# The states' output stage of a hybrid encoder layer: its u and Toeplitz loads by four groups into four buffers

## The chip, the core and the metric

The kernel runs on one core of a Trainium2 chip. A core has five engines that run side by side, each with its own stream of instructions: TensorE (PE, matrix products; PEld are its weight loads), VectorE (DVE), ScalarE (ACT), GpSimd (POOL) and SyncE (SP). Transfers between the chip's main memory and the on-chip memory go through 16 DMA engines that all of the core's queues share. POOL, SP and ACT issue them; each has a queue of its own. The metric is the device time of one execution in microseconds (us).

## The reference

One encoder layer over two sequences of 512 tokens with 1024 channels, all in float32. Two branches start from the same normalised rows: a windowed attention, and a state-space branch (S5) with 64 groups of 16 channels and 64 complex states per group and direction. A merge and an MLP follow.

```
h = rms_norm(x, ln1)
q, k, v, u, g_att, g_ssm = split(h @ w_in)
y_att = windowed_attention(rms_norm(q), rms_norm(k), v, sink, bias, mask)
# per direction d and group g, a linear recurrence over the tokens:
#   state[l] = a * state[l-1] + b_bar @ u[l];   y[l] = Re(c @ state[l])
y = y_forward + y_backward + d_skip * u
y = gelu(y);  y_ssm = y * sigmoid(y @ w_glu + b_glu)
mixed = sigmoid(g_att) * y_att + sigmoid(g_ssm) * y_ssm
x = x + mixed @ w_out
out = x + square(relu(rms_norm(x, ln2) @ w_up)) @ w_down
```

## The kernel before

The kernel is one long program for one core. Most of its time goes into matrix products, written as three products of split operands. The state-space branch works in blocks of 8 tokens. Within a block, the output follows from the inputs through a Toeplitz block per group (128 x 128); what comes from earlier blocks goes through the states at the block's edge. So the branch has three stages:

1. Coefficients. `tables` makes, by 8 groups, the tables `ct_scr` (from states to outputs) and the lags of the Toeplitz blocks, and stores them in main memory. Eight transfers (L595) build `toep_scr` from the lags.
2. The recurrence over the blocks, on DVE (L619 to L625). PE meanwhile works on the columns of the input projection; `pull` takes so many units of them at a time.
3. The states' output stage (L644 to L673), which the change is about. It has 32 steps `q` of `SH` = 2 groups. For each group, PE multiplies the Toeplitz block `toep` with the inputs `u_sb` (L655) and adds two products of the table `ctab` with the states `st` (L658). ACT applies the GELU (L665) and stores the outputs by four groups (L640). Behind each step, `pull` puts some matmuls of the projection (L185) or of the keys (L225) on PE.

Three kinds of tiles are loaded from main memory for the output stage, all issued by POOL. `u_sb` (L601) and `toep` (L603) are loaded for `SB` = 8 groups at a time, 512 KB each, into two buffers each. `ctab_in` (L609) is loaded for `SI` = 4 groups, 512 KB, into three buffers. Two of the first kind and three of the second are loaded ahead of the recurrence (L613 to L615). Behind them stands a copy of 4 MB in main memory, `line_scr` (L616), for the attention's biases. In the loop, a load is asked for when the last step that uses its buffer has been written (L670 to L673). I call the four groups of one `ctab` a set: it has two steps, and there are 16.

The orders of PE, ACT and DVE in this stage are those in which the code is written (`manual_schedule`, L618). POOL isn't among them there: a scheduler sets its order. A load waits until PE has read what stood in its buffer, and until an older transfer of POOL's queue that used the same semaphore (there are eight, in turn) has landed. Behind these loads on POOL stand the key norms, L238 and L239, on which DVE's L242 waits.

Of the kernel before, what the change touches and what calls it, by code (L numbers as in the profile page):

```python
# [12 lines left out]
F32 = mybir.dt.float32  # L13
# [6 lines left out]
P = 128  # L20
# [5 lines left out]
NSEQ = 2  # L26
# [12 lines left out]
GROUPS = 64  # L39
STATE = 64  # L40
CH = 16
T = 8
NCHUNK = SEQ // T
SB = 8
SI = 4
SG = 4
SH = 2
# [16 lines left out]
def hybrid_layer(ctx, tc, x, rel, onehot, w_qkv, w_ug, vectors, lam, coefs, w_glu, w_out, ln2,  # L64
                 w_up, w_down, out):
    nc = tc.nc
    V, S, PE, GP, SP = nc.vector, nc.scalar, nc.tensor, nc.gpsimd, nc.sync
# [18 lines left out]
    def sps():  # L86
        return ps_s.tile([P, 512], F32, tag="sps", name="sps")

    u_scr = dram.tile([GROUPS, CH, T, NSEQ * NCHUNK], F32, name="u_scr")
# [3 lines left out]
    toep_scr = dram.tile([CH, T, GROUPS, T * CH], F32, name="toep_scr")  # L93
# [173 lines left out]
    def pull(units):  # L267
        while units > 0:
            cost = next(filler, None)
            if cost is None:  # L270
                return
            units -= cost
            phase["units"] -= cost
# [175 lines left out]
    with tc.tile_pool(name="hst", bufs=1) as hp:  # L449
# [147 lines left out]
        with tc.tile_pool(name="ssmo", bufs=2) as sp:  # L597
            def load_batch(g0):

                u_sb = sp.tile([P, SB, NSEQ * NCHUNK], F32, tag="u_sb", name="u_sb")  # L600
                GP.dma_start(u_sb, u_scr[g0:g0 + SB].rearrange("g c t k -> (c t) g k"))  # L601
                toep = sp.tile([P, SB, T, CH], F32, tag="toep", name="toep")
                GP.dma_start(toep.rearrange("p g t c -> p g (t c)"),  # L603
                             toep_scr[:, :, g0:g0 + SB].rearrange("c t g n -> (c t) g n"))
                return u_sb, toep

            def load_table(g0):
                ctab = sp.tile([P, SI, 2, T * CH], F32, tag="ctab", name="ctab_in", bufs=3)
                GP.dma_start(ctab.rearrange("p g r n -> p (g r n)"),  # L609
                             ct_scr[:, g0:g0 + SI].rearrange("p g r n -> p (g r n)"))  # L610
                return ctab

            ahead = [load_batch(0)]  # L613
            ahead_c = [load_table(0), load_table(SI), load_table(2 * SI)]
            ahead.append(load_batch(SB))  # L615
            GP.dma_start(line_scr, line_one[:, None, :].to_broadcast([N_HEADS, P, LINE]))  # L616
            order.close()
            order.enter_context(tc.manual_schedule(engines={mybir.EngineType.PE, mybir.EngineType.Activation, mybir.EngineType.DVE}))  # L618
            for i in range(1, NCHUNK - 1):  # L619
                t1, t2 = [sp.tile([P, 2, GROUPS, NSEQ], F32, tag="st", name=n, bufs=3) for n in ("t1", "t2")]  # L620
                V.tensor_mul(t1, h[:, i], a8r)
                V.tensor_mul(t2, h[:, i, ::-1], a8i)
                V.tensor_add(t1, t1, h[:, i + 1])
                V.tensor_add(h[:, i + 1], t1, t2)
                pull(15)  # L625
            phase["gelu"] = True
            pull(64)
            def state_rows(q):
                st = sp.tile([P, 2, SH, NSEQ, NCHUNK], F32, tag="st", name="st", bufs=3)
                hv = h[:, :, :, q * SH:(q + 1) * SH, :].rearrange("p k r g s -> p r (g s) k")  # L630
                sv = st.rearrange("p r g s k -> p r (g s) k")
                V.tensor_copy(sv[64:128], hv[64:128, :, :, ::-1])
                if q % 2 == 0:
                    S.copy(sv[0:64], hv[0:64])
                else:
                    V.tensor_copy(sv[0:64], hv[0:64])
                return st

            def store_y(y, ga):
                S.dma_start(y_scr[:, :, ga:ga + SI].rearrange("t c g k -> (t c) (g k)"), y.rearrange("p g k -> p (g k)"))  # L640

            states = [state_rows(0), state_rows(1)]
            full = None
            for q in range(GROUPS // SH):  # L644
                g0 = q * SH
                if g0 % SB == 0:
                    u_sb, toep = ahead.pop(0)
                if g0 % SI == 0:
                    ctab = ahead_c.pop(0)
                    ys = sp.tile([P, SI, NSEQ * NCHUNK], F32, tag="ys", name="ys", bufs=3)  # L650
                st = states.pop(0)
                ps = sps()
                for g in range(SH):
                    o = ps[:, g * P:(g + 1) * P]
                    PE.matmul(o, toep[:, g0 % SB + g].rearrange("p t c -> p (t c)"), u_sb[:, g0 % SB + g, :],  # L655
                              start=True, stop=False)
                    for ri in range(2):
                        PE.matmul(o, ctab[:, g0 % SI + g, ri, 0:T * CH],  # L658
                                  st[:, ri, g].rearrange("p s k -> p (s k)"), start=False, stop=ri == 1)
                if q + 2 < GROUPS // SH:  # L660
                    states.append(state_rows(q + 2))
                if full:
                    store_y(*full)
                    full = None
                S.activation(ys[:, g0 % SI:g0 % SI + SH].rearrange("p g k -> p (g k)"), ps[:, 0:SH * P], AF.Gelu_apprx_tanh)  # L665
                if (g0 + SH) % SI == 0:
                    full = ys, g0 + SH - SI

                pull(-(-(phase["units"] - 84) // (GROUPS // SH - q)))
                if (g0 + SH) % SI == 0 and g0 + SH + 2 * SI < GROUPS:  # L670
                    ahead_c.append(load_table(g0 + SH + 2 * SI))
                if (g0 + SH) % SB == 0 and g0 + SH + SB < GROUPS:
                    ahead.append(load_batch(g0 + SH + SB))  # L673
            store_y(*full)
            pull(phase["units"])
            order.close()
# [67 lines left out]
    with tc.tile_pool(name="att", bufs=2, reuse_waits="tile") as ap, tc.tile_pool(name="attc", bufs=1, reuse_waits="tile") as ac:  # L744
# [293 lines left out]
        with tc.manual_schedule(engines={ET.PE, ET.Activation, ET.DVE, ET.Pool}):  # L1038
            for i, (j, sq) in enumerate(steps):
# [4 lines left out]
                for qb in range(NB):  # L1044
                    if 1 <= i < 3:
                        t = (i - 1) * NB + qb
# [599 lines left out]
```

## Time and profile before

| what | value |
| --- | --- |
| time, three runs | 1472.97, 1475.15, 1476.32 us; median 1475.15 |
| profiled execution, first to last instruction (span) | 1471.1 us |
| profiled execution, time besides its span | not given by the page; the median lies 4.05 us above the span |
| PE busy in the span | 1442.0 us |
| mean granted TensorE clock | 0.999 |
| bytes moved by DMA | 234.48 MB, mean 159 GB/s |
| output stage | about 325 to 405 us |

In the page's row for an engine stand its busy time, its share of the span and its instructions. A row of the windows view has a stretch of the span, its length, the busy time of PE, PEld, DVE, ACT and POOL, the granted clock (1.00 is full), the mean busy share of the DMA engines, and GB/s. In the timeline a row has its start, its length, the engine, the line, the operation, what it writes and reads, and in brackets the idle time ahead of it and what ended that. One of the program's float32 products stands there as two matmuls. A row of the waits view has who waited for what: us in total, times, longest.

What PE does in the stretches that the change bears on is shown with the prediction, next to the argument that uses it.

### The profile page before, as it was taken

The page shows a single profiled execution, that of the slowest core. Times are in us where ns is not written, and L with a number is a line of the kernel's source. Part 1 is how long each engine was busy: PE and PEld are TensorE (multiplying, and loading weights), DVE is VectorE, ACT ScalarE, POOL GpSimd, SP SyncE. Part 2 cuts the span into 40 slices and gives each one's busy share as a digit, 9 for nine tenths or more (in the row PEclk, how much of TensorE's full clock was granted, in tenths as well). Part 3 has the DMA queues.
Part 4 walks back from the last instruction along what each step waited for, and adds up shares of the span by engine and source line. Part 5 has one row for each costly group of instructions (what it writes and reads, how often), then busy time and mean ns, then how long its engine had stood idle before and what let it go on. Part 6 is the DMA issues. An engine that isn't in the chain of part 4 may idle for free.

```text
span 1471.1 us, 22069 instructions
## 1 busy us (share of the span) xinstructions
PE 1442.0 (98%) x8074; PEld 1230.7 (84%) x8074; DVE 1092.2 (74%) x1965; ACT 754.9 (51%) x1346; POOL 226.8 (15%) x372
## 2 busy tenths in 40 slices
PE   6999999999999999999999999999999999999998
PEld 4888888888999999987888878888888878888787
DVE  7989849995446899988985587777776597475553
ACT  6678852234336888786343355454454444333332
POOL 3044451003332442252100000000000000000000
PEclk9999999999999999999999999999999999999999
DMA  4455559428630533345552255444442993454441
GB/s 177 137 165 174 159 157 339 144 100 288 234 135 24 172 104 106 105 150 177 182 192 102 86 169 174 149 146 154 145 146 108 339 330 103 158 184 147 126 130 58
DMA packets 98269, 234.48 MB, mean 159 GB/s; under 512 B 11722, under 2 KB 23242, under 8 KB 98160
## 3 DMA queue, kind: packets, MB, share of 16 engines
q1 hardware_dynamic: 59088, 135.35, 28.5%
q0 software_dynamic: 15744, 47.23, 9.9%
q10 hardware_dynamic: 23328, 50.47, 9.4%
q8 instruction: 64, 1.05, 0.3%
q14 instruction: 45, 0.37, 0.1%
HBM read 163.78 MB, written 80.77 MB: 166 GB/s over the span
## 4 chain that ended last, share of the span: by engine, by line
PE 74%; DVE 12%; DMA 4%; issue 4%; ACT 4%; POOL 2%; SPq 0%; DVEq 0%; ACTq 0%; POOLq 0%
PE bank L117 14%; PE bank L118 13%; PE bank L116 13%; PE acc L185 6%; PE acc L821 5%; PE acc L117 3%; PE acc L118 3%; PE acc L116 3%; PE acc L123 2%; DMA c_raw<-in_w_ug_dram 2%; PE sps L553 2%; PE po L904 2%; PE sps L872 2%; PE tps L888 2%; PE acc L225 1%
## 5 line engine op out<-in xcount | busy, mean ns | idle before, releaser
L185 PE MATMUL acc<-act,c_hi 128*128 128x512 f32 x768 | 244.2, 396 | 1.0 <-DVE act L311 1.0
L117 PE MATMUL bank<-b_lo,a_hi 128*128 128x512 f32 x448 | 174.6, 390 | 2.3 <-DVE b_lo L1515 2.3
L118 PE MATMUL bank<-b_hi,a_lo 128*128 128x512 f32 x448 | 174.3, 389 | 0.0
L116 PE MATMUL bank<-b_hi,a_hi 128*128 128x512 f32 x448 | 173.5, 389 | 0.0
L185 PEld LDWEIGHTS acc<-act,c_hi 128*128 128x128 f32 x768 | 143.0, 189 | 30.4 <-DVE act L311 2.4
L1514 ACT CAST a_hi<-d_a 128x1024 fp32r<-128x1024 f32 x56 | 59.0, 1054 | 180.5 <-PE bank L117 177.1
L185 PE MATMUL acc<-act,c_lo 128*128 128x512 f32 x384 | 151.0, 393 | 0.0
L116 PE MATMUL bank<-act,act 128*128 128x512 f32 x368 | 143.3, 389 | 0.5 <-ACT f_sum L1339 0.5
L117 PE MATMUL bank<-act,act 128*128 128x512 f32 x368 | 143.3, 389 | 0.2 <-DVE act L1298 0.2
L118 PE MATMUL bank<-act,act 128*128 128x512 f32 x368 | 143.2, 389 | 0.0
L1515 DVE TENSOR_TENSOR a_lo<-d_a,a_hi 128x1024 fp32r<-128x1024 f32 x56 | 68.5, 1224 | 98.5 <-ACT a_hi L1514 98.5
L821 PE MATMUL acc<-w_hi,act 128*128 128x256 f32 x512 | 114.1, 291 | 0.0
L117 PEld LDWEIGHTS bank<-b_lo,a_hi 128*128 128x128 f32 x448 | 84.1, 188 | 20.7 <-DVE b_lo L1515 3.3
L116 PEld LDWEIGHTS bank<-b_hi,a_hi 128*128 128x128 f32 x448 | 84.1, 188 | 17.6
L118 PEld LDWEIGHTS bank<-b_hi,a_lo 128*128 128x128 f32 x448 | 84.1, 188 | 17.4
L821 PEld LDWEIGHTS acc<-w_hi,act 128*128 128x128 f32 x512 | 87.1, 190 | 3.7
L185 PEld LDWEIGHTS acc<-act,c_lo 128*128 128x128 f32 x384 | 72.3, 188 | 14.7 <-DVE c_lo L176 0.4
L882 ACT ACTIVATE p<-p,nmx 128x257 f32<-128x257 f32 (+1 forms) x128 | 72.1, 564 | 19.7 <-DVE nmx L876 17.6
L116 PEld LDWEIGHTS bank<-act,act 128*128 128x128 f32 x368 | 69.1, 188 | 15.4 <-ACT f_sum L1339 0.9
L117 PEld LDWEIGHTS bank<-act,act 128*128 128x128 f32 x368 | 69.1, 188 | 14.8 <-DVE act L1298 0.5
L123 PE MATMUL acc<-act,gc_hi 128*128 128x512 f32 x256 | 81.2, 394 | 0.0
L118 PEld LDWEIGHTS bank<-act,act 128*128 128x128 f32 x368 | 69.1, 188 | 14.2
(333 smaller groups left out, 3425.1 us busy)
## 6 DMA issues: line engine op xcount, KB each, us to landing
d_a<-a_scr SPq DMA_DIRECT2D x56, 512.0 KB, 3.8
raws<-in_w_up_dram SPq DMA_DIRECT2D x32, 512.0 KB, 4.0
a_scr<-t ACTq DMA_DIRECT2D x64, 256.0 KB, 2.9
k<-in_w_down_dram SPq DMA_DIRECT2D x32, 512.0 KB, 5.9
c_raw<-in_w_ug_dram SPq DMA_DIRECT2D x48, 256.0 KB, 3.8
ct_scr<-ctab POOLq DMA_DIRECT2D x16, 512.0 KB, 4.7
ctab_in<-ct_scr POOLq DMA_DIRECT2D x16, 512.0 KB, 7.3
a_scr<-a ACTq DMA_DIRECT2D x32, 256.0 KB, 2.0
```

The costliest lines, as they stand in the source:

```text
L116: PE.matmul(ps, a[0], b[0], start=first, stop=False)
L117: PE.matmul(ps, a[0], b[1], start=False, stop=False)
L118: PE.matmul(ps, a[1], b[0], start=False, stop=last)
L123: PE.matmul(ps, w[wi][:, k, :], rows[yi], start=k + p == 0, stop=k == KT - 1 and p == 2)
L185: PE.matmul(ps, w[wi][:, k, :], hT[s][hi][:, k, :], start=n == 0, stop=n == 3 * KT - 1)
L553: PE.matmul(ps[:, i * P:(i + 1) * P], bm[:, ri, g, :], u_sb[:, gp * SH + g, :], start=True, stop=True)
L821: PE.matmul(self.ps, hT[sq][act][:, k, col:col + P], w[:, k % 4, :], start=i == 0, stop=i == 3 * KT - 1)
L872: PE.matmul(ps[:, 0:self.nk], qs, kk[:, self.k0 * P:self.k1 * P], start=i == 0, stop=i == 1)
L882: S.activation(p, p, AF.Exp, bias=self.nmx[:, h:h + 1], scale=-1.0, accum_out=self.sums[:, h, self.qb:self.qb + 1])
L888: PE.transpose(pt[:, h * P:(h + 1) * P], self.p[:, h, 1 + i * P:1 + (i + 1) * P], ident)
L1514: S.copy(hi, src)
L1515: V.tensor_sub(lo, src, hi.bitcast(F32))
```

## The change

`load_batch` loads four groups, not eight, and its two tiles have four buffers, not two. The memory that they take is the same. In the loop, a new `u_sb` and `toep` are taken at each set, and the next are loaded after each set, four sets ahead. The first loads are asked for in the order in which they are used: `u_sb`, `toep` and `ctab` of set 0, then of 1, then of 2, then `u_sb` and `toep` of set 3. The lines from L613 on move by one or two in the listing.

```diff
             def load_batch(g0):
 
-                u_sb = sp.tile([P, SB, NSEQ * NCHUNK], F32, tag="u_sb", name="u_sb")
-                GP.dma_start(u_sb, u_scr[g0:g0 + SB].rearrange("g c t k -> (c t) g k"))
-                toep = sp.tile([P, SB, T, CH], F32, tag="toep", name="toep")
+                u_sb = sp.tile([P, SI, NSEQ * NCHUNK], F32, tag="u_sb", name="u_sb", bufs=4)
+                GP.dma_start(u_sb, u_scr[g0:g0 + SI].rearrange("g c t k -> (c t) g k"))
+                toep = sp.tile([P, SI, T, CH], F32, tag="toep", name="toep", bufs=4)
                 GP.dma_start(toep.rearrange("p g t c -> p g (t c)"),
-                             toep_scr[:, :, g0:g0 + SB].rearrange("c t g n -> (c t) g n"))
+                             toep_scr[:, :, g0:g0 + SI].rearrange("c t g n -> (c t) g n"))
                 return u_sb, toep
...
-            ahead = [load_batch(0)]
-            ahead_c = [load_table(0), load_table(SI), load_table(2 * SI)]
-            ahead.append(load_batch(SB))
+            ahead, ahead_c = [], []
+            for g0 in range(0, 3 * SI, SI):
+                ahead.append(load_batch(g0))
+                ahead_c.append(load_table(g0))
+            ahead.append(load_batch(3 * SI))
...
-                if g0 % SB == 0:
+                if g0 % SI == 0:
                     u_sb, toep = ahead.pop(0)
-                if g0 % SI == 0:
                     ctab = ahead_c.pop(0)
...
-                    PE.matmul(o, toep[:, g0 % SB + g].rearrange("p t c -> p (t c)"), u_sb[:, g0 % SB + g, :],
+                    PE.matmul(o, toep[:, g0 % SI + g].rearrange("p t c -> p (t c)"), u_sb[:, g0 % SI + g, :],
...
-                if (g0 + SH) % SB == 0 and g0 + SH + SB < GROUPS:
-                    ahead.append(load_batch(g0 + SH + SB))
+                if (g0 + SH) % SI == 0 and g0 + SH + 3 * SI < GROUPS:
+                    ahead.append(load_batch(g0 + SH + 3 * SI))
```

On POOL, the first loads stand behind the eight transfers that build `toep_scr`. Before:

```order
L595 DMA toep_scr<-lag_scr 16x64x128 x8
L601 DMA u_sb<-u_scr 128x8x128
L603 DMA toep<-toep_scr 128x1024
L609 DMA ctab_in<-ct_scr 128x1024 x3
L601 DMA u_sb<-u_scr 128x8x128
L603 DMA toep<-toep_scr 128x1024
L616 DMA line_scr<-line_one 2048x1x512
L609 DMA ctab_in<-ct_scr 128x1024 x2
```

At the same place on POOL, now:

```order
L595 DMA toep_scr<-lag_scr 16x64x128 x8
L601 DMA u_sb<-u_scr 128x4x128
L603 DMA toep<-toep_scr 128x512
L609 DMA ctab_in<-ct_scr 128x1024
L601 DMA u_sb<-u_scr 128x4x128
L603 DMA toep<-toep_scr 128x512
L609 DMA ctab_in<-ct_scr 128x1024
L601 DMA u_sb<-u_scr 128x4x128
L603 DMA toep<-toep_scr 128x512
L609 DMA ctab_in<-ct_scr 128x1024
L601 DMA u_sb<-u_scr 128x4x128
L603 DMA toep<-toep_scr 128x512
```

The copy of `line_scr` follows behind the last of these rows, as L618. The sizes show the halves: 128x4x128 in place of 128x8x128, and 128x512 in place of 128x1024.

Near the end of the loop, the key norms come between the loads on POOL. Before, from the loads for the last eight groups but one to the last table:

```order
L601 DMA u_sb<-u_scr 128x8x128
L609 DMA ctab_in<-ct_scr 128x1024
L603 DMA toep<-toep_scr 128x1024
L609 DMA ctab_in<-ct_scr 128x1024
L238 TENSOR_SCALAR ms<-ms 128x4
L239 TENSOR_TENSOR rk<-ms,neg_half 128x4
L601 DMA u_sb<-u_scr 128x8x128
L609 DMA ctab_in<-ct_scr 128x1024
L603 DMA toep<-toep_scr 128x1024
L238 TENSOR_SCALAR ms<-ms 128x4
L239 TENSOR_TENSOR rk<-ms,neg_half 128x4
L609 DMA ctab_in<-ct_scr 128x1024
```

On POOL, now, at the same place:

```order
L601 DMA u_sb<-u_scr 128x4x128
L609 DMA ctab_in<-ct_scr 128x1024
L238 TENSOR_SCALAR ms<-ms 128x4
L603 DMA toep<-toep_scr 128x512
L239 TENSOR_TENSOR rk<-ms,neg_half 128x4
L601 DMA u_sb<-u_scr 128x4x128
L609 DMA ctab_in<-ct_scr 128x1024
L603 DMA toep<-toep_scr 128x512
L238 TENSOR_SCALAR ms<-ms 128x4
L239 TENSOR_TENSOR rk<-ms,neg_half 128x4
L609 DMA ctab_in<-ct_scr 128x1024
```

Each table now has a `u_sb` ahead of it and a `toep` behind it; before, every second table stood alone. One `toep` load has moved between L238 and L239. PE, DVE, ACT and SP have the same instructions in the same order as before.

## The prediction

> **What bounds the kernel now.** I read the busy line first, then the stretches by window, then what TensorE waited for, then the starts of the steps in the stage that the change touches.
>
> ```profile
> span 1471.1 us, 22069 instructions
> PE 1442.0 (98%) x8074; PEld 1230.7 (84%) x8074; DVE 1092.2 (74%) x1965; ACT 754.9 (51%) x1346; POOL 226.8 (15%) x372
> ```
>
> TensorE (PE) is busy for 1442.0 of 1471.1 us. A change in loads can only win what PE loses waiting for them, or what a lower clock costs behind such a wait. So the next question is how much of that lies in the states' output stage.
>
> ```profile
> 201.00:325.00 124.00, 124.00 (x607) 102.83 (x596) 106.61 (x271) 30.66 (x51) 17.65 (x28) 1.00 0.57 196
> 325.00:405.00 80.00, 75.72 (x569) 71.63 (x568) 42.86 (x61) 34.96 (x61) 26.82 (x33) 0.98 0.74 247
> ```
>
> The columns are the stretch, its length, then busy us of PE, PEld, DVE, ACT and POOL, the granted clock, the DMA share and GB/s. In 201 to 325 us (first loads and state recurrence) PE has no hole. In 325 to 405 us, the output stage, it loses 80 − 75.72 = 4.3 us and the granted clock is 0.98. The waits of PE in 201 to 405 us are two:
>
> ```profile
> PE sps L655 <- DMA toep<-toep_scr: 2.9, 2, 2.1
> PE sps L658 <- ACT st L634: 1.4, 1, 1.4
> ```
>
> The second is the first step's wait for its states; the change doesn't touch it. The first is the one at stake: two waits of L655 for the Toeplitz blocks. The timeline of PE shows them at the first L655 of a step (a step is one `q`: two groups, two L655 pairs), with the idle time in brackets:
>
> ```profile
> 361.44 0.38 PE L655 MATMUL sps<-u_sb,toep 128*128 128x128 f32 x2
> ...
> 364.65 0.46 PE L655 MATMUL sps<-u_sb,toep 128*128 128x128 f32 x2 [0.78 <-DMA toep<-toep_scr]
> ...
> 380.69 0.39 PE L655 MATMUL sps<-u_sb,toep 128*128 128x128 f32 x2
> ...
> 385.30 0.46 PE L655 MATMUL sps<-u_sb,toep 128*128 128x128 f32 x2 [2.15 <-DMA toep<-toep_scr]
> ...
> 389.01 0.60 PE L655 MATMUL sps<-u_sb,toep 128*128 128x128 f32 x2
> ...
> 391.53 0.39 PE L655 MATMUL sps<-u_sb,toep 128*128 128x128 f32 x2
> ...
> 393.82 0.39 PE L655 MATMUL sps<-u_sb,toep 128*128 128x128 f32 x2
> ```
>
> An undisturbed step takes 393.82 − 391.53 = 2.29 us. Against that, the step that ends in the first wait took 3.21 (0.92 too long), the one that ends in the second 4.61 (2.32 too long), and the two behind it 3.71 and 2.52 (1.42 and 0.23 too long). The last two aren't waits. The window there shows why:
>
> ```profile
> 386.00:389.00 3.00, 3.00 (x16) 3.00 (x16) 0.18 (x1) 0.77 (x2) 0.00 (x0) 0.51 1.01 352
> ```
>
> The granted clock was 0.51 for these 3 us, right behind the hole. So the lateness of `toep` costs 0.92 + 2.32 + 1.42 + 0.23 = **4.9 us**.
>
> [...]
>
> **Why toep comes late.** The timeline of POOL shows the loads for the eight groups that the second wait is about (steps 24 to 27), and the chain of waits how long the last of them took:
>
> ```profile
> 372.87 0.91 POOL L601 DMA_DIRECT2D u_sb<-u_scr  x1 [3.44 <-PE sps L655]
> 373.77 0.72 POOL L609 DMA_DIRECT2D ctab_in<-ct_scr  x1
> 374.49 0.77 POOL L603 DMA_DIRECT2D toep<-toep_scr  x1
> ```
>
> ```profile
> 374.49 10.68 DMA toep<-toep_scr
> ```
>
> `u_sb` waits until step 19 has read the old buffer. `toep` is issued 1.6 us later, behind `u_sb` and `ctab_in`, and is due at step 24, that is at 380.69 + 2.29 = 382.98. It has 8.5 us and takes 10.7. The loads of this kind in 330 to 395 us, all x6, and the tables, x13:
>
> ```profile
> L603 POOL DMA_DIRECT2D toep<-toep_scr x6: 531/531/766, 337.4 to 384.1; - x6
> ...
> DMA to landing us min/median/max: 7.2/8.5/10.7
> ```
>
> ```profile
> L609 POOL DMA_DIRECT2D ctab_in<-ct_scr x13: 531/641/803, 330.9 to 391.7; - x13
> ...
> DMA to landing us min/median/max: 4.3/7.1/9.4
> ```
>
> The median landing of `toep`, 8.5 us, equals the time that it has. Every such load is on the edge; two of six fell over it. Transfers are slow because the DMA engines are near full here:
>
> ```profile
> 335.00:340.00 5.00, 5.00 (x37) 4.63 (x37) 2.30 (x3) 1.76 (x3) 2.09 (x3) 1.00 0.58 170
> ...
> 332.00:385.00 53.00, 50.37 (x374) 46.85 (x372) 28.71 (x39) 23.93 (x42) 19.66 (x25) 1.00 0.91 307
> ```
>
> **The change part by part.** The built order of PE, DVE, ACT and SP holds the same instructions in the same places; only POOL's differs. So every term is a matter of when a load is issued and lands.
>
> *Halves into four buffers.* A load for four groups (a set, two steps) goes into a buffer that the set four before it has freed, and is due when three more sets are done: 3 x 2 x 2.29 = 13.7 us after the release, against 4 x 2.29 = 9.2 us before. The new order issues `u_sb`, `ctab_in`, `toep` as before, so `toep` stands some 1.6 us behind the release again (less, if half a load takes less time to issue) and has about 12.1 us. It took at most 10.7 at twice the size. So no wait of L655 on `toep` or `u_sb` is left, by a margin of 1.4 us even over the worst row: **−4.9 us**. If only a part of the lateness goes, for instance the 0.92, that is the lower bound of this term; the upper is the 4.9, as PE has no other loss that these loads cause.
>
> *The bytes.* They are the same, so a longer lead helps only if the queue isn't overrun. A set needs 0.52 MB of `u_sb` and `toep`, 0.52 of `ctab_in`, and its output store 0.26: 1.31 MB in 4.58 us, or 286 GB/s; the 53 us above moved 307 with a share of 0.91, so 337 at a full share is my estimate of the ceiling. Demand is below it, but not by much, and what decides is the start. POOL's timeline has the first loads of the loop:
>
> ```profile
> 330.86 0.65 POOL L609 DMA_DIRECT2D ctab_in<-ct_scr  x1 [91.93 <-PE acc L185]
> ...
> 336.47 0.92 POOL L601 DMA_DIRECT2D u_sb<-u_scr  x1
> ```
>
> The table went out when set 0 was done, `u_sb` only after set 1, and the DMA share of 335 to 340 us was 0.58. Now set 4's `u_sb` and `toep` go out beside that table, near 331 us, and take room that lay idle. That is half a megabyte moved out of the crowded part, 1.6 us of its time at 307 GB/s.
>
> *More DMAs.* 16 loads become 32, that is 16 issues more on POOL:
>
> ```profile
> L601 POOL DMA_DIRECT2D u_sb<-u_scr x6: 907/1184/1454, 336.5 to 382.1; - x6
> ```
>
> With this row and that of `toep` they take 0.53 to 1.45 us each, 9 to 23 us in all if each costs as much as a whole one now. POOL is busy 19.7 of the 53 us above and off the path, so this costs nothing unless it delays `ctab_in`, which is below. In the transfer itself a half may cost more than half: between nothing and the whole of the POOL issue, 0.53 us per extra DMA, two to a set. The queue's own rows say which is near:
>
> ```profile
> q0 software_dynamic: 3029, 11.04, 64.3%
> ```
>
> 11.04 MB are 21 loads of 0.52 MB in the 53 us, 2.5 us for each, while one takes 7 to 8.5 to land: three are in flight at once, and a fixed part of one lies beside the data of the next. I take nothing.
>
> *`ctab_in`* keeps its three buffers and its lead of two sets. But a `u_sb` now stands ahead of it at every set, not at every second, though half as large: one issue, 0.9 us, later at each second set. In the row of the tables the longest landing is 9.4 us. That was the one issued at 373.77, behind a whole `u_sb`, and due at 383.3 (0.3 behind step 24's L655), so it had 9.5. This is the next one late. With half a `u_sb` ahead of it, and half a megabyte less in the crowd, I expect 1 to 2 us less. I take nothing here as well, and price the failure as a rival.
>
> *What waits on POOL.* Its `u_sb` issue waits for PE, now at twelve sets in place of six; behind it stand `ctab_in`, `toep` and, at the last sets, the key norms' L238 and L239, on which DVE's L242 waits. One `toep` now stands between L238 and L239 (0.53 us). DVE has cover: it is busy 28.7 of the 53 us. Without it the cost would be 0.5 us once.
>
> *First loads.* They now go out by set, and the copy of `line_scr` behind them can wait for an older load's landing. They are done about 60 us ahead of their use at 325, beside a stretch in which PE is busy 124.00 of 124 us, so nothing. What could lose its cover are the column weights of that stretch, which come through the same engines; moving the copy by one landing, 10.7 us at the longest, changes the crowd, not the bytes. Between nothing and one hole like the larger one above (2.3 us), I take nothing, since PE shows no wait there.
>
> **Sum.** The span becomes 1471.1 − 4.9 = 1466.2 us. The page gives no other time of the profiled execution; the runs' median, 1475.15, is 4.05 us above the span. I carry this over: **1470.25 us**, 0.33% faster. About 0.2%, 3 us, is what a measurement here can tell from no change.
>
> **Rivals.**
>
> *A. `ctab_in` takes over part of the wait.* To step 24's use of set 12's table, the DMA engines must move, from the first packets at about 332: tables 3 to 12 (5.2 MB), 19 halves of `u_sb` and `toep` (5.0), eleven output stores (2.9), and 2.1 of other columns' loads and stores: 15.2 MB. The due time without the first stall is 382.3. [...] A table that is 1.3 us late leaves 3.6 us of the win; if the clock drops behind it as above (1.65), 1.95. Time 1471.5 to 1473.2. For it: the 9.4 us row. Against it: no wait for a table in the rows of before. 18%.
>
> *B. Nothing to win in the timed executions.* The two waits are 0.8 and 2.1 us in one execution, and six loads lie within about 2 us of their due time, so they vary; the three times of before span 1472.97 to 1476.32. If most timed executions lose only about 1 us here, or the change does what it says and another wait fills the place, the time is 1473.5 to 1476. 19%.
>
> *C. Slower: the smaller transfers slow the queue, and `ctab_in` (L609), with its short lead, stalls PE at set after set.* To eat the whole 4.9 us, table 12 must be 3.3 us late with the clock's 1.65 behind it, so through at 385.6: 15.2 MB in 53.3 us, or 285 GB/s. Below that mean rate it is slower; at 270 it is 6.3 us late, 7.9 with the clock, minus 4.9: 1478 us. Against it: 307 GB/s in the row, and the overlap of three in flight. 8%.
>
> [...]
>
> **How the numbers follow.** Forecast 55%, A 18%, B 19%, C 8%. Faster by over 0.2% (below 1472.2): the forecast and a third of A, 0.61. Slower by over 0.2% (above 1478.1 or near it): C, 0.08, at most. The same: 0.31. The range leaves out C and the outer edge of B above, and below only what the runs' own spread of 1.7 us around the median can add: 1468.5 to 1475.5.
>
> **What would show it.** In the profile after: the waits of PE have no row of L655 on `toep`; the granted clock of 380 to 395 us is 1.00; steps are 2.29 us apart through the stage, which ends 4.9 us earlier; loads start near 331 us and the DMA share of 335 to 340 rises above 0.58. Rival A shows as a row of L658 on `ctab_in`, near step 24. The forecast is wrong if PE waits anew there, if the clock drops without a hole, or if the DMA rate of the stage falls below 300 GB/s.

## The result and the profile after

| | before | after |
| --- | --- | --- |
| time, median of 22 runs each | 1472.47 us (1469.15 to 1476.35) | 1469.54 us (1468.25 to 1472.36) |
| ratio, 95% interval | | 0.9983 (0.9976 to 0.9990) |
| profiled execution | 1472.97 us, span 1471.1 | 1471.88 us, span 1470.1 |

The forecast was 1470.25 us. The time lies 0.7 us below it and inside the range. The gain came out smaller: it is 2.9 us (0.17% by the ratio), not 4.9. It lies just inside the 0.2% that I had named as the bound of what can be told from no change. With 22 runs of each, the interval still excludes no change. The three runs of before had a median of 1475.15; 22 runs have 1472.47. A base that was 2.7 us too high and a gain that was 2.0 us too large nearly cancelled.

The page after, its span and busy line:

```profile
span 1470.1 us, 22100 instructions
PE 1441.8 (98%) x8074; PEld 1230.4 (84%) x8074; DVE 1092.2 (74%) x1965; ACT 755.3 (51%) x1346; POOL 237.1 (16%) x388
```

The waits of PE in 201 to 405 us, after; it is the only row:

```profile
PE sps L659 <- ACT st L636: 1.9, 1, 1.9
```

The waits on `toep` (2.9 us in two) are gone, and no wait for a table came. (Lines moved by one or two: L655 is L656 now, L658 is L659, L634 is L636, the copy L616 is L618.) The windows of after, with the columns of the prediction:

```profile
201.00:325.00 124.00, 124.00 (x608) 102.80 (x607) 105.90 (x270) 31.03 (x51) 19.94 (x32) 1.00 0.57 196
325.00:405.00 80.00, 78.13 (x592) 74.34 (x591) 44.33 (x64) 35.67 (x62) 34.81 (x45) 0.98 0.74 253
335.00:340.00 5.00, 5.00 (x36) 4.59 (x36) 2.31 (x3) 1.88 (x4) 1.96 (x4) 1.00 0.83 259
332.00:385.00 53.00, 53.00 (x397) 49.93 (x396) 29.14 (x40) 25.18 (x44) 27.36 (x37) 1.00 0.90 303
385.00:390.00 5.00, 5.00 (x46) 5.00 (x46) 2.98 (x6) 2.35 (x5) 3.28 (x5) 1.00 1.00 365
328.30:331.70 3.40, 3.40 (x13) 3.01 (x13) 3.06 (x5) 1.25 (x2) 0.00 (x0) 0.50 0.32 103
```

From 332 to 385 us PE has no hole (before: 2.6 us), and the clock of 385 to 390 is full. The share of the DMA engines in 335 to 340 rose from 0.58 to 0.83. Yet the whole stage still has a granted clock of 0.98: the last row shows a new place at half clock. It lies right behind the wait for the states. PE's timeline there, after:

```profile
325.56 0.38 PE L656 MATMUL sps<-u_sb,toep 128*128 128x128 f32 x2
327.81 0.77 PE L659 MATMUL sps<-st,ctab_in 128*128 128x128 f32 x4 [1.87 <-ACT st L636]
...
331.76 0.38 PE L656 MATMUL sps<-u_sb,toep 128*128 128x128 f32 x2
```

The same step before:

```profile
324.97 0.38 PE L655 MATMUL sps<-u_sb,toep 128*128 128x128 f32 x2
326.71 0.68 PE L658 MATMUL sps<-st,ctab_in 128*128 128x128 f32 x4 [1.36 <-ACT st L634]
...
329.06 0.38 PE L655 MATMUL sps<-u_sb,toep 128*128 128x128 f32 x2
```

The first step, with its two groups, took 331.76 − 325.56 = 6.20 us, before 329.06 − 324.97 = 4.09: 2.11 more. Of these 0.51 are the longer hole (1.87 against 1.36); the other 1.60 are the half clock. The account of the two profiled spans: the stage's start +0.59, the first step +2.11, the next 30 steps −5.0, the last step and all behind it +1.3. That is −1.0 us, 1471.1 to 1470.1. Of the +1.3, 0.5 is one wait of PE near 1209 us (L117 for DVE's `b_lo`: 1.63 us, before 1.14). In the profiles of all the kernels it lies between 0.37 and 1.69 us.

### The profile page after: what moved, and what is told of

It reads as the page before. It is cut to its first block, busy times and chain, and to the rows that moved or that the text cites. A ratio compares the mean times of both kernels' runs of the same rounds, so it can differ in the third digit from the quotient of the medians.

```text
span 1470.1 us, 22100 instructions
## 1 busy us (share of the span) xinstructions
PE 1441.8 (98%) x8074; PEld 1230.4 (84%) x8074; DVE 1092.2 (74%) x1965; ACT 755.3 (51%) x1346; POOL 237.1 (16%) x388
## 4 chain that ended last, share of the span: by engine, by line
PE 77%; DVE 12%; DMA 4%; ACT 4%; issue 2%; POOL 1%; SPq 0%; DVEq 0%; ACTq 0%; POOLq 0%
PE bank L117 13%; PE bank L118 13%; PE bank L116 13%; PE acc L185 7%; PE acc L822 5%; PE acc L117 3%; PE acc L118 3%; PE acc L116 3%; DMA c_raw<-in_w_ug_dram 2%; PE acc L123 2%; PE sps L659 2%; PE sps L553 2%; PE po L905 2%; PE sps L873 2%; PE acc L225 2%
## 5 line engine op out<-in xcount | busy, mean ns | idle before, releaser
L117 PE MATMUL bank<-b_lo,a_hi 128*128 128x512 f32 x448 | 174.7, 390 | 2.9 <-DVE b_lo L1516 2.8
L117 PE MATMUL bank<-act,act 128*128 128x512 f32 x368 | 143.3, 389 | 0.2 <-DVE act L1299 0.2
L117 PEld LDWEIGHTS bank<-b_lo,a_hi 128*128 128x128 f32 x448 | 84.1, 188 | 21.9 <-DVE b_lo L1516 4.5
L117 PEld LDWEIGHTS bank<-act,act 128*128 128x128 f32 x368 | 69.1, 188 | 14.8 <-DVE act L1299 0.5
```

Source lines behind the costliest of these rows:

```text
L117: PE.matmul(ps, a[0], b[1], start=False, stop=False)
```

## The experiments

The first question was what had removed the waits: the longer lead, the smaller loads, or the order of the first loads (theory L: lateness of `toep`, removed by lead or size; its rivals: the order did it, or there is more to win). The second was why so little arrived. I suspected the hole at the first step (theory H: the loads by halves use up the eight semaphores of POOL's queue, so the copy of `line_scr` waits for an older load; it goes out late and crowds the column weights that DVE waits for in the midst of its recurrence).

Each kernel was timed in five rounds; a ratio is to the kernel before in the same rounds, with its 95% interval. "Hole" is the idle time of PE ahead of the first step's state products in the profiled execution.

**The changed kernel once more** (no edit).

> The changed kernel once more, for a second profile. Theory L (the late toep loads were the loss; with a lead of three sets they land in time): no wait of L655/L656 on toep or u_sb, all steps after the first two 2.26 to 2.50 us apart. Theory H (the column weights that the copy of line_scr delays hold up DVE, so the hole at the first step grew from 1.36 to 1.87 us and let the clock drop): the copy is issued near 243 us again, DVE waits for c_hi by 0.7 us or more at two columns between 250 and 270 us, and the hole before the first step's table product is 1.7 to 2.0 us; the clock may drop behind it or not. Rival R (the larger hole was chance): the hole is 1.2 to 1.5 us. Time 0.1 to 0.3% below the kernel before.

1470.69 us, ratio 0.9986 (0.9974 to 0.9999), hole 1.89 us, half clock behind it again. So a second profile of the same kernel shows the same hole. But DVE's waits were not where theory H had them: 1.96 us at 234 us, and only 0.27 and 0.29 between 250 and 270, where 0.7 or more at two columns was expected. Each run also lists its mean granted clock to three digits. Of 35 runs of before in these rounds, 19 have 1.000 and a mean time of 1470.70 us, and 16 have less and 1474.04. Of the 12 of after, 3 have 1.000 and 1470.05, and 9 have less and 1470.81. A drop of 3.41 us to half clock takes 0.001 off that mean, so a run at 1.000 has no drop. A run at less need not have one in its midst: the profiled execution of the next kernel but one, halves_three, has 0.999, with a granted clock of 1.00 in 325 to 405 us. In the profile of after, a second half clock begins at 1468.33 us, behind the last product, which ends at 1466.29. So before has a drop in at most about half of its executions. Its runs at less than 1.000 are some 3 us longer, and one drop accounts for about 1.6 of that; the rest isn't shown. Where neither kernel has a drop, before is only about 1 us slower than after (0.65 here; 1.2 against the 1469.51 of the first 16 runs of after at 1.000).

**No loads in the loop.** The reloads of `u_sb` and `toep` are left out; the four first buffers are used in turn.

> Leaves out the twelve reloads of u_sb and toep in the loop: later sets are computed with the first four sets' tiles, so 6.3 MB less is moved in the stage. Theory L: the changed kernel has nothing left to win from these loads, so the time is within 0.5 us of the changed kernel's. Rival (crowding still costs the changed kernel something, by tables or weights that land late): 1 us or more below it.

```diff
+            kept = list(ahead)
...
-                    ahead.append(load_batch(g0 + SH + 3 * SI))
+                    ahead.append(kept[(g0 + SH + 3 * SI) // SI % 4])
```

1469.39 us, ratio 0.9983 (0.9970 to 0.9995); after had 1470.69 and 0.9986 in the same rounds. The intervals don't tell the two apart. By the ratios, 0.0003 apart, this is theory L's row; by the medians, 1.3 us apart, it is the rival's. So it isn't settled whether some 1 us of crowding by these loads is left.

**Halves, but three buffers.**

> Loads by four groups, but three buffers: lead of two sets, 9.1 us from release to use, as long as the eights in two buffers have. Theory L by lead alone (the lead is what counts): waits of PE on toep come back, one to three of them, 0.5 to 2.5 us in all, time 1 to 4 us above the changed kernel's. Rival S (size is what counts: halves land sooner, 5 to 7.5 us, so 9.1 is enough): no wait on toep, time within 0.7 us of the changed kernel's.

```diff
-                u_sb = sp.tile([P, SI, NSEQ * NCHUNK], F32, tag="u_sb", name="u_sb", bufs=4)
+                u_sb = sp.tile([P, SI, NSEQ * NCHUNK], F32, tag="u_sb", name="u_sb", bufs=3)
...
-                toep = sp.tile([P, SI, T, CH], F32, tag="toep", name="toep", bufs=4)
+                toep = sp.tile([P, SI, T, CH], F32, tag="toep", name="toep", bufs=3)
...
-            ahead.append(load_batch(3 * SI))
...
-                if (g0 + SH) % SI == 0 and g0 + SH + 3 * SI < GROUPS:
-                    ahead.append(load_batch(g0 + SH + 3 * SI))
+                if (g0 + SH) % SI == 0 and g0 + SH + 2 * SI < GROUPS:
+                    ahead.append(load_batch(g0 + SH + 2 * SI))
```

1470.16 us, ratio 0.9985 (0.9975 to 0.9996); the short lead of before (two sets, 9.2 us) with half the size. PE's wait on `toep` in its profile (the only other in 201 to 405 us is the hole at the first step):

```profile
PE sps L655 <- DMA toep<-toep_scr: 0.4, 1, 0.4
```

One wait of 0.4 us is left of 2.9. That lies between theory L (0.5 us or more) and rival S (none), nearer to S. Landing of a `toep` load in 330 to 395 us, this kernel and then after:

```profile
DMA to landing us min/median/max: 4.8/6.7/8.9
```

```profile
DMA to landing us min/median/max: 5.0/6.6/9.1
```

Before it was 7.2/8.5/10.7. The halves land about 1.9 us sooner, and that alone brings them nearly all inside the old lead. The hole at the first step was 0.22 us here.

**Eights, but three buffers** (a longer lead alone).

> Loads by eight groups as before the change, but three buffers (16 KB more per partition pair of tiles): lead of four sets, 18.3 us. Theory L by lead: no wait on toep, the stage's steps as in the changed kernel. Rival S (size): the eights still land late in the crowd, waits on toep of 0.5 us or more remain.

```diff
-                u_sb = sp.tile([P, SB, NSEQ * NCHUNK], F32, tag="u_sb", name="u_sb")
+                u_sb = sp.tile([P, SB, NSEQ * NCHUNK], F32, tag="u_sb", name="u_sb", bufs=3)
...
-                toep = sp.tile([P, SB, T, CH], F32, tag="toep", name="toep")
+                toep = sp.tile([P, SB, T, CH], F32, tag="toep", name="toep", bufs=3)
...
+            ahead.append(load_batch(2 * SB))
...
-                if (g0 + SH) % SB == 0 and g0 + SH + SB < GROUPS:
-                    ahead.append(load_batch(g0 + SH + SB))
+                if (g0 + SH) % SB == 0 and g0 + SH + 2 * SB < GROUPS:
+                    ahead.append(load_batch(g0 + SH + 2 * SB))
```

The edit is to the kernel before the change. 1471.03 us, ratio 0.9992 (0.9980 to 1.0004). No wait on `toep`, though its landing has a median of 7.8 us and a longest of 9.7. So the lead alone removes the waits too; the time is not told from that of before, with a hole of 1.95 us and half clock behind it.

**Order alone**: eights in two buffers as before, first loads in the order of use.

> The other part alone: eights in two buffers as before the change, first loads in order of use. Theory L: waits on toep of 0.7 us or more at one to three steps, as before the change; the time is that of the kernel before within 1 us. Theory H: the copy goes out near 238 us (no semaphore to wait for), hole at the first step 1.3 to 1.5 us.

```diff
-            ahead = [load_batch(0)]
-            ahead_c = [load_table(0), load_table(SI), load_table(2 * SI)]
-            ahead.append(load_batch(SB))
+            ahead, ahead_c = [], []
+            for g0 in range(0, 3 * SI, SI):
+                if g0 % SB == 0:
+                    ahead.append(load_batch(g0))
+                ahead_c.append(load_table(g0))
```

This edit, too, is to the kernel before. 1472.73 us, ratio 1.0001 (0.9991 to 1.0010). The copy went out at 238.39 us, and the hole is 1.34 us, as expected. Its PE waits in 201 to 405 us, and a window:

```profile
PE sps L657 <- DMA toep<-toep_scr: 2.9, 1, 2.9
PE sps L660 <- ACT st L636: 1.3, 1, 1.3
```

```profile
385.00:389.00 4.00, 3.26 (x15) 3.29 (x16) 0.00 (x0) 0.32 (x1) 0.00 (x0) 0.57 0.93 317
```

The wait and the low clock are back at the place of before. The order of the first loads alone wins nothing that can be told.

**Halves in four buffers, the old order of first loads.**

> The changed kernel with the first loads in the old order: sets 0 and 1 of u_sb and toep, three tables, sets 2 and 3, the copy. The copy still waits for an older load's semaphore. Theory H: it is issued no sooner than in the changed kernel (243 us, give or take 1), DVE waits for c_hi as there, the hole is 1.7 to 2.0 us; the order of the first loads alone is worth nothing, within 0.5 us. Rival (the order of use itself moved the hole): hole 1.3 to 1.5 us.

```diff
-            for g0 in range(0, 3 * SI, SI):
-                ahead.append(load_batch(g0))
-                ahead_c.append(load_table(g0))
-            ahead.append(load_batch(3 * SI))
+            ahead = [load_batch(0), load_batch(SI)]
+            ahead_c = [load_table(0), load_table(SI), load_table(2 * SI)]
+            ahead += [load_batch(2 * SI), load_batch(3 * SI)]
```

1468.89 us, ratio 0.9976 (0.9965 to 0.9987): the gain comes without the new order. The hole is 2.07 us, with half clock behind it; so the new order didn't make the hole either. The copy went out at 241.55 us, 2.1 us sooner than in after, and the hole is no smaller for it.

**The copy of `line_scr` ahead of all first loads.**

> The copy of line_scr is asked for ahead of the first loads instead of behind them. It is issued near 220 us and is through before 250. Theory H: the columns' weights in 245 to 270 us land sooner, DVE has less waiting for c_hi in the recurrence than the 2.4 us of the changed kernel (but maybe more near 235), and the hole at the first step changes with it, by as much as the sum of these waits. If the sum falls by 0.5 us, the hole is 1.3 to 1.4 us. Rival R: the hole stays at 1.8 to 1.9 whatever DVE waited.

1471.59 us, ratio 0.9997 (0.9986 to 1.0008). The copy went out at 219.32 us, and no gain over before can be told. Waits of PE in 201 to 405 us:

```profile
PE sps L659 <- ACT st L636: 1.7, 1, 1.7
PE acc L185 <- DVE c_lo L176: 0.9, 2, 0.6
```

The column weights come late enough here that PE itself stops for them twice. So the copy does compete with the column weights, and its place counts. DVE's waits didn't fall, as theory H had it: they rose to 4.39 us, and the hole is 1.74 us. This run says nothing yet of a copy that goes out only a little sooner.

**The copy one place further up**, ahead of the load of set 3, so that it waits for no load.

> After, with the copy of line_scr put one place further up, ahead of the load of the states' set 3. If the copy that goes out late is what lengthens the hole at the states' first step (theory H): it goes out near 238.4 us, as in the three-buffer kernel, VectorE's recurrence has no wait on c_lo behind 250 us, the hole ahead of the first step is at most 1.4 us (after: 1.87), no half clock follows it, and the time is 1 to 2.5 us below after's. If the hole has another cause (rival): the hole stays at 1.8 to 2.0 us wherever the copy goes out, and the time is within 0.7 us of after's.

```diff
-            ahead.append(load_batch(3 * SI))
             GP.dma_start(line_scr, line_one[:, None, :].to_broadcast([N_HEADS, P, LINE]))
+            ahead.append(load_batch(3 * SI))
```

POOL's timeline of after, where the last first loads and the copy each wait for the load issued eight places ahead of them:

```profile
239.74 0.76 POOL L601 DMA_DIRECT2D u_sb<-u_scr  x1 [1.20 <-DMA toep<-toep_scr]
241.78 0.55 POOL L603 DMA_DIRECT2D toep<-toep_scr  x1 [1.28 <-DMA ctab_in<-ct_scr]
243.64 1.05 POOL L618 DMA_DIRECT2D line_scr<-line_one  x1 [1.31 <-DMA u_sb<-u_scr]
```

The same in this kernel:

```profile
238.47 1.06 POOL L617 DMA_DIRECT2D line_scr<-line_one  x1
```

The copy went out 5.2 us sooner, as meant (before: 237.86). But DVE still waits for the column weights behind 250 us. Its timeline in this kernel, and then in after:

```profile
233.62 0.69 DVE L176 TENSOR_TENSOR c_lo<-c_raw,c_hi 128x512 fp32r<-128x512 f32 x1 [1.35 <-ACT c_hi L175]
...
266.66 0.69 DVE L176 TENSOR_TENSOR c_lo<-c_raw,c_hi 128x512 fp32r<-128x512 f32 x1 [1.03 <-ACT c_hi L175]
```

```profile
233.65 0.69 DVE L176 TENSOR_TENSOR c_lo<-c_raw,c_hi 128x512 fp32r<-128x512 f32 x1 [0.79 <-ACT c_hi L175]
...
255.71 0.69 DVE L176 TENSOR_TENSOR c_lo<-c_raw,c_hi 128x512 fp32r<-128x512 f32 x1 [0.75 <-ACT c_hi L175]
...
267.30 0.69 DVE L176 TENSOR_TENSOR c_lo<-c_raw,c_hi 128x512 fp32r<-128x512 f32 x1 [0.89 <-ACT c_hi L175]
```

The hole is 1.75 us, and the time 1470.32 us, ratio 0.9992 (0.9983 to 1.0001). That is the rival's row, not H's: **theory H fell in its last step**. A late copy is not what makes the hole.

What holds across the kernels is the link from DVE's waits to the hole. The table adds up DVE's waits at L176 behind 214 us:

| kernel | `u_sb` and `toep` loaded first | DVE waits, us | hole, us | half clock right behind it |
| --- | --- | --- | --- | --- |
| halves_three | 6 loads, 1.5 MB | 0.82 | 0.22 | no |
| before | 4 loads, 2 MB | 2.00 | 1.36 | no |
| eights_in_order | 4 loads, 2 MB | 2.34 | 1.34 | no |
| copy_fourth | 8 loads, 2 MB | 2.38 | 1.75 | no |
| after | 8 loads, 2 MB | 2.43 | 1.87 | yes |
| after_again | 8 loads, 2 MB | 2.52 | 1.89 | yes |
| eights_three | 6 loads, 3 MB | 2.50 | 1.95 | yes |
| no_reload | 8 loads, 2 MB | 2.75 | 2.04 | no |
| halves_old_order | 8 loads, 2 MB | 2.65 | 2.07 | yes |

In eight of the nine the hole is DVE's waits less 0.55 to 0.71 us; eights_in_order is off by 0.4. So the recurrence, with these waits in it, ends last ahead of the first step. The chain of waits of after runs the same way: from two loads of column weights through the recurrence to ACT's `st` and to PE's L659. The two loads, with start and length:

```profile
244.98 10.05 DMA c_raw<-in_w_ug_dram
256.42 10.20 DMA c_raw<-in_w_ug_dram
```

In before's chain the loads at these two places took 9.55 and 8.63 us.

The kernels with two MB in eight loads have 1.75 to 2.07 us, those with the same bytes in four loads 1.34 and 1.36. That fits a cost of about 0.5 us for the split. The bytes may count as well: 1.5 MB goes with the smallest hole, 3 MB with one of the larger. With one profile of most kernels, and with nothing that shows how the split delays the weights, this is an argument and not shown. copy_first isn't in the table. There PE's own work waited as well (0.92 us), and a hole of 1.74 us beside 4.39 us of DVE's waits doesn't fit the relation.

**Fill the hole.** Ahead of the stage, `pull(64)` puts 64 units of the projection on PE. These kernels take 80 or 96, and so fewer in the stage; nothing else is changed, or the copy's place as above.

```diff
-            pull(64)
+            pull(80)
```

> The changed kernel with 8 more products of the projection (16 units) ahead of the first step and so fewer between the steps: 8 x 0.227 = 1.8 us of work laid into the hole at the first step. Theory H's second half (the hole and the clock behind it are what is left of the loss in this stage): hole below 0.3 us, no drop of the clock near 328 us, time 1.4 to 3.5 us below the changed kernel's. Rival (the hole is set by DVE's and ACT's work behind PE, and moves to the next steps, as the steps get shorter): PE waits on st at later steps, and the time gains less than 0.7 us.

1468.43 us, ratio 0.9973 (0.9963 to 0.9983). The hole is 0.95 us: half as long, but not under 0.3 as expected. No half clock follows it. After itself wasn't timed in these rounds.

> After with pull(96) alone. H: of the hole of 0.95 us that pull(80) left under 0.3 us is left, and the time is up to 0.9 us below that of pull(80). Rival: the work that is kept back delays something behind the stage, and the time is no better than with pull(80).

1467.54 us, ratio 0.9972 (0.9964 to 0.9981); by the intervals that isn't told from `pull(80)`. PE's timeline and window show no hole:

```profile
328.54 0.39 PE L185 MATMUL acc<-act,c_hi 128*128 128x512 f32 x1
328.77 0.38 PE L656 MATMUL sps<-u_sb,toep 128*128 128x128 f32 x2
328.99 0.61 PE L659 MATMUL sps<-st,ctab_in 128*128 128x128 f32 x4
```

```profile
325.00:405.00 80.00, 80.00 (x625) 76.72 (x624) 45.28 (x66) 36.29 (x64) 36.80 (x49) 1.00 0.80 272
```

PE is busy for 80.00 of 80 us, at full clock. DVE's waits are still there (2.39 us); they cost nothing, since PE has work in their place.

> The same with 80 filling matmul groups' due time in place of 64 (pull(80)). H: what is left of the hole after the earlier copy is filled, under 0.5 us, and this is the fastest so far, 1467 to 1468.5 us, ratio to before near 0.997. Rival: the filling work is missing further back, waits turn up at later steps on the states' rows, and the time is that of fill_80 or above it.

(96 and 80 are units of `pull`, as said above.) 1468.07 us, ratio 0.9972 (0.9960 to 0.9984), nine runs. Its hole is 0.95 us, not under 0.5: this expectation missed in its first part, and the earlier copy added nothing to `pull(80)` that can be told.

> The earlier copy and pull(96). H: hole 0, time equal to copy_fourth_fill within 0.5 us, since nothing is left to fill. Rival: slower than pull(80) by what the kept-back work delays elsewhere.

1466.84 us, ratio 0.9966 (0.9954 to 0.9978), five runs: no hole in the stage. It is the lowest median, but not told apart from `fill_96` (`pull(96)` alone) by the intervals. It lies 1.2 us below copy_fourth_fill, where no more than 0.5 was expected. In these rounds copy_fourth alone had 1470.32, so filling its hole is worth 2.3 to 3.5 us by the medians. Against after only the ratios to before can be compared, from different rounds: 0.9983 and 0.9986 there, 0.9973 and 0.9972 with `pull(80)` and `pull(96)`. That is 1.5 to 2 us.

## Why the prediction was right or wrong

- **`toep`'s lateness and its cure: right.** All waits on `toep` and `u_sb` went, and a load now takes at most 9.1 us of a lead of 13.7. Either part does it: the smaller load leaves one wait of 0.4 us, the longer lead none. The rows I had said would show it are there: the steps, 2.29 us apart in PE's timeline of after:

```profile
384.61 0.39 PE L656 MATMUL sps<-u_sb,toep 128*128 128x128 f32 x2
...
386.90 0.39 PE L656 MATMUL sps<-u_sb,toep 128*128 128x128 f32 x2
...
389.19 0.39 PE L656 MATMUL sps<-u_sb,toep 128*128 128x128 f32 x2
```

- **The 4.9 us: right for that one execution, wrong as what an execution loses.** The 30 steps behind the first are 5.0 us shorter in the profile of after. But over many executions before loses less against after: about 1 us where neither has a clock drop, and some 3 us more where the mean clock is below 1.000, in about half. This was rival B's mechanism in a milder form; I gave it 19% as a case by itself, where it should have scaled the term.
- **"I carry this over", 4.05 us outside the span: wrong.** In all the runs of the later rounds the time is 1.72 to 1.85 us above the span. The profiled execution was the fastest of the three, 1472.97 us, and its other 2.2 us were the distance from that run to a median of three. The forecast's span of 1466.2 with 1.8 around it would have said 1468.0.
- **"First loads ... nothing": the failed step.** The hole behind the recurrence was 0.5 us larger, with half clock behind it: 2.1 us in the profile of after, put at nothing in the sum. I took nothing "since PE shows no wait there". PE did not, but DVE did, and its recurrence had little slack at its end: by the table about 0.6 us. My range for the term, up to 2.3 us, held it, and I had named the column weights as what could lose its cover. The way I gave for it, the copy moved by one landing, was wrong: it moved by 5.8 us, but its being moved back didn't close the hole.
- **Smaller steps.** Bytes and rate: right, 303 GB/s against 307. "Near 331 us": the loads of set 4 went out at 333.56 to 334.95, late by the 2.7 us that the stage's start and first step had lost:

```profile
333.56 0.65 POOL L609 DMA_DIRECT2D ctab_in<-ct_scr  x1 [88.86 <-PE acc L185]
334.20 0.77 POOL L601 DMA_DIRECT2D u_sb<-u_scr  x1
334.95 0.54 POOL L603 DMA_DIRECT2D toep<-toep_scr  x1
```

  For the same reason the last step starts only 2.3 us earlier (400.66 us, before 403.00), not 4.9. Rival A: no wait on `ctab_in`; its landing fell to 3.9/6.1/8.6 us from 4.3/7.1/9.4. Five loads of before in 330 to 396 us, with nothing else of their queue under way at their end, landed 0.3 to 0.4 us behind their last packet. Rival C: no. Its sum leaves that time out, and from 332 to 385.6 are 53.6 us, not 53.3; neither changes what it says. No run here shows a loss at 256 KB in the loop: `toep` landed sooner (a median of 6.6 us, before 8.5), and the rate was about the same (303 GB/s, before 307).
- **Still open:** what delays the column weights at 234, 255 and 267 us (a kernel without the copy of `line_scr` wasn't tried), whether the split in halves is what lengthens the hole, and 0.8 of the +1.3 us behind the stage between the two profiles, which other executions may not share.

## What to carry to other kernels

Size a gain by many executions, not by one profile: a wait for a load that is on the edge varies, and in some executions a clock drop comes on top of it (1.65 us on 2.32 in the profile of before). Where an engine shows no wait in a stretch, look at the engine that it will wait for at the stretch's end, before you price an extra load there at nothing. And where such a wait at a seam can't be removed, put work there whose order you are free to choose: 32 more units ahead of the seam closed a hole whose cause stayed open.

## What the hardware showed that I had not expected

Half clock followed holes in PE shorter than the drop itself. The drop lasted 3.41 us at a clock of 0.50 (328.28 to 331.69 us in after, 386.05 to 389.46 in before). It came behind holes of 1.87 (after), 1.89 (after_again), 1.95 (eights_three), 2.07 (halves_old_order), 2.15 (before) and 2.85 us (eights_in_order). It did not come behind 1.34 (eights_in_order), 1.36 (before), 1.74 (copy_first) and 1.75 (copy_fourth), nor behind one of 2.04 (no_reload). The stretch with the hole and the one with the drop, in after:

```profile
324.86:328.28 3.42, 1.55 (x10) 1.25 (x9) 3.35 (x7) 2.44 (x3) 0.00 (x0) 1.00 0.18 51
328.28:331.69 3.41, 3.41 (x13) 3.02 (x13) 3.08 (x5) 1.27 (x2) 0.00 (x0) 0.50 0.33 105
```

The end of the hole and what follows it, first in no_reload (2.04 us), then in halves_old_order (2.07 us):

```profile
327.00:331.00 4.00, 3.88 (x28) 3.69 (x29) 3.62 (x6) 1.84 (x3) 0.00 (x0) 1.00 0.35 126
```

```profile
327.00:331.00 4.00, 3.94 (x15) 3.55 (x16) 3.61 (x5) 1.78 (x3) 0.00 (x0) 0.57 0.37 119
```

So a hole of about 2 us cost a clock drop in one execution and none in another. Its length alone doesn't decide it, as 1.87 us was followed by a drop and 2.04 was not; what does is not shown.

POOL's own loads hold each other back at issue: in after, three in a row each stood 1.2 to 1.3 us, each on the landing of the load eight places ahead. The copy behind them went out 5.8 us later than before, 3.8 us of it in these three waits.
